# Row variances on one Trainium2 core: larger first loads, smaller last pieces, and part of one column loaded over 15 to 1 partitions

## Chip, cores and metric

The kernel runs on one core of a Trainium2 chip. The metric is the device time of one execution in microseconds; lower is better. Three runs of the kernel before took 165.55, 165.44 and 165.35 us, median 165.44 us. One more execution was recorded by the hardware profiler; its trace is what the rest is read from.

## What is computed

```python
# x: float32 (32, 512, 1024)
mean_sq = np.mean(x**2, axis=-1)
sq_mean = np.mean(x, axis=-1)**2
return (mean_sq - sq_mean).astype(np.float32)     # (32, 512)
```

So each of 16384 rows of 1024 floats gives its variance. The input has 67.11 MB and must be read once; the output has 0.07 MB.

## The kernel before, in words

The rows are laid out as 128 columns: a column is one row of 1024 floats (4 KB) in each of the 128 partitions. Columns 0 to 15 are the first 2048 rows of x (each partition holds 16 rows that follow one another in memory), columns 16 to 127 are the rest (112 rows that follow one another). A load of n columns therefore reads n x 4 KB in one stretch for each partition. All loads are issued by SyncE (SP) through `load` (L40, the DMA at L45).

**Loads.** Columns 0 to 103 come in 13 loads of 8 columns into three rotating buffers `xt` (L145); a load into a buffer in use waits for the engines that still read it. Columns 104 to 127 have a buffer of their own, `xt_end` (L73), and come in loads of 6, 6, 4, 3, 2 and 1 columns (`END_LOADS`) and then, for the last two columns, in four half columns of 2 KB a partition (L173 to L179). Loads use eight completion semaphores in turn, so that a load also waits for the one eight DMAs earlier. The two stores of results are DMAs too: the one for columns 0 to 15 goes out from ScalarE (ACT), L181, the one for the rest from SP at the end, L182.

**Work.** A column goes to one of two engines. VectorE (DVE) takes two `bn_stats` of 512 floats (L111), each of which leaves two records of count, mean and sum of squared deviations (six floats). ACT takes two passes of 1024 floats: a Copy that sums the row into `neg_mean` (L121) and a Square with that mean as its bias, which sums into the result (L129); each ends with a read of its accumulator. Of 8 columns ACT takes 3 or 2 in turn, of the last 24 those marked A in `END_WHO`. What ACT writes besides sums goes to `junk`, bf16 in SBUF.

**Joining records.** For the body and for the first two loads of the end, GpSimd (POOL) joins the DVE's records of many columns at once (`join`, L81 to L108). For later columns DVE does it itself, one `bn_aggr` a column (L169, L179). Each engine's instructions run in the order written; the framework adds the waits on semaphores.

Of the kernel before, what the change touches and what calls it, by code (L numbers as in the profile page):

```python
# [10 lines left out]
@with_exitstack  # L11
def kernel(
    ctx: ExitStack,
    tc: tile.TileContext,
    x: bass.AP,
    out: bass.AP,
):

    nc = tc.nc
    P = nc.NUM_PARTITIONS
    FP32 = mybir.dt.float32
    ACTF = mybir.ActivationFunctionType
    ALU = mybir.AluOpType

    xf = x.flatten_outer_dims()
    N, D = xf.shape
    assert N % P == 0
    ncols = N // P  # L30
    H = D // 2


    SMALL = 16
    BLOCKS = [(0, SMALL, 0), (SMALL, ncols - SMALL, SMALL * P)]

    def block_of(c):
        return next(b for b in BLOCKS if b[0] <= c < b[0] + b[1])

    def load(dst, c0, n, f0=0, f=D):  # L40

        b0, pitch, row0 = block_of(c0)
        assert c0 + n <= b0 + pitch
        ap = [[pitch * D, P], [D, n], [1, f]] if n > 1 else [[pitch * D, P], [1, f]]
        nc.sync.dma_start(  # L45
            out=dst,
            in_=dataclasses.replace(xf, offset=(row0 + c0 - b0) * D + f0, ap=ap),
        )

    def store(engine, block):  # L50
        b0, pitch, row0 = block
        engine.dma_start(
            out=dataclasses.replace(out, offset=row0, ap=[[pitch, P], [1, pitch]]),
            in_=mv[:, 1, b0 : b0 + pitch],
        )

    GROUP = 8
    NGROUPS = 13
    END0 = GROUP * NGROUPS
    ACT_OF_GROUP = (3, 2)  # L60

    END_LOADS = [6, 6, 4, 3, 2, 1]
    END_WHO = "AADDDDAADDDDDADDDADADA"
    BATCH = (2, 6, 2)

    xpool = ctx.enter_context(tc.tile_pool(name="xpool", bufs=3))
    spool = ctx.enter_context(tc.tile_pool(name="spool", bufs=4))
    opool = ctx.enter_context(tc.tile_pool(name="opool", bufs=1))

    mv = opool.tile([P, 2, ncols], FP32)  # L70
    neg_mean = opool.tile([P, ncols], FP32)
    junk = [opool.tile([P, D], mybir.dt.bfloat16, name=f"junk{i}") for i in range(4)]
    xt_end = opool.tile([P, ncols - END0, D], FP32)  # L73
    stats_of = {}

    def stats_block(name, groups, each):

        st = opool.tile([P, groups * each, 2, 6], FP32, name=name)
        return st

    def join(st, groups, each, first, step, skip):  # L81

        n = groups * each
        part = st.rearrange("p n h (e s) -> p n (h e) s", s=3)
        mean, m2 = part[:, :, :, 1], part[:, :, :, 2]
        two = opool.tile([P, n, 2], FP32, name=f"two{first}")
        mu = opool.tile([P, n, 1], FP32, name=f"mu{first}")
        dev = opool.tile([P, n, 4], FP32, name=f"dev{first}")
        g = nc.gpsimd
        g.tensor_tensor(out=two, in0=mean[:, :, 0:2], in1=mean[:, :, 2:4], op=ALU.add)  # L90
        g.tensor_tensor(out=mu, in0=two[:, :, 0:1], in1=two[:, :, 1:2], op=ALU.add)
        g.tensor_scalar(out=mu, in0=mu, scalar1=0.25, scalar2=None, op0=ALU.mult)  # L92
        g.tensor_tensor(out=dev, in0=mean, in1=mu.to_broadcast([P, n, 4]), op=ALU.subtract)  # L93
        g.tensor_tensor(out=dev, in0=dev, in1=dev, op=ALU.mult)  # L94
        g.tensor_scalar(out=dev, in0=dev, scalar1=D / 4.0, scalar2=None, op0=ALU.mult)  # L95
        g.tensor_tensor(out=dev, in0=dev, in1=m2, op=ALU.add)  # L96
        g.tensor_tensor(out=two, in0=dev[:, :, 0:2], in1=dev[:, :, 2:4], op=ALU.add)  # L97
        g.tensor_tensor(out=mu, in0=two[:, :, 0:1], in1=two[:, :, 1:2], op=ALU.add)
        var = mv[:, 1, first : first + groups * step].rearrange(
            "p (g k) -> p g k", k=step  # L100
        )[:, :, skip : skip + each]
        g.tensor_scalar(  # L102
            out=var,
            in0=mu.rearrange("p (g k) o -> p g (k o)", k=each),
            scalar1=1.0 / D,
            scalar2=None,
            op0=ALU.mult,
        )  # L108

    def dve_half(stats, h, xh):  # L110
        nc.vector.bn_stats(out=stats[:, h, :], in_=xh)  # L111

    def dve_halves(stats, xcol):
        dve_half(stats, 0, xcol[:, :H])
        dve_half(stats, 1, xcol[:, H:])

    def act_cols(cols):

        s = D ** -0.5
        for i, (xcol, c) in enumerate(cols):  # L120
            nc.scalar.activation(  # L121
                out=junk[i],
                in_=xcol,
                func=ACTF.Copy,
                scale=-s / D,
                accum_out=neg_mean[:, c : c + 1],
            )
        for i, (xcol, c) in enumerate(cols):
            nc.scalar.activation(  # L129
                out=junk[3],  # L130
                in_=xcol,
                func=ACTF.Square,
                scale=s,
                bias=neg_mean[:, c : c + 1],
                accum_out=mv[:, 1, c : c + 1],
            )

    body = []
    for par in range(2):
        groups = len(range(par, NGROUPS, 2))  # L140
        each = GROUP - ACT_OF_GROUP[par]
        body.append((stats_block(f"stats{par}", groups, each), groups, each))
    for g in range(NGROUPS):
        c0 = g * GROUP
        xt = xpool.tile([P, GROUP, D], FP32, name="xt")  # L145
        load(xt, c0, GROUP)
        skip = ACT_OF_GROUP[g % 2]
        act_cols([(xt[:, k, :], c0 + k) for k in range(skip)])
        st, _, each = body[g % 2]
        for k in range(skip, GROUP):  # L150
            dve_halves(st[:, g // 2 * each + k - skip, :, :], xt[:, k, :])
    for par, (st, groups, each) in enumerate(body):
        join(st, groups, each, par * GROUP, 2 * GROUP, ACT_OF_GROUP[par])

    nb, step, skip = BATCH
    each = step - skip
    st_end = stats_block("stats_end", nb, each)
    k = 0
    for b, n in enumerate(END_LOADS):
        load(xt_end[:, k : k + n, :] if n > 1 else xt_end[:, k, :], END0 + k, n)  # L160
        mine = range(k, k + n)
        act_cols([(xt_end[:, j, :], END0 + j) for j in mine if END_WHO[j] == "A"])
        for j in mine:
            if END_WHO[j] == "D" and b < nb:
                dve_halves(st_end[:, b * each + j - k - skip, :, :], xt_end[:, j, :])
            elif END_WHO[j] == "D":
                stats = spool.tile([P, 2, 6], FP32, name="stats")
                dve_halves(stats, xt_end[:, j, :])
                nc.vector.bn_aggr(out=mv[:, :, END0 + j], in_=stats)  # L169
        if b == nb - 1:  # L170
            join(st_end, nb, each, END0, step, skip)
        k += n
    for j in range(k, ncols - END0):  # L173
        stats = spool.tile([P, 2, 6], FP32, name="stats")
        for h in range(2):
            xh = xt_end[:, j, h * H : (h + 1) * H]
            load(xh, END0 + j, 1, h * H, H)
            dve_half(stats, h, xh)
        nc.vector.bn_aggr(out=mv[:, :, END0 + j], in_=stats)  # L179

    store(nc.scalar, BLOCKS[0])  # L181
    store(nc.sync, BLOCKS[1])  # L182
# [30 lines left out]
```

## Time and profile before

| what | value | from |
|---|---|---|
| median of three runs | 165.44 us | times |
| span of the profiled execution | 163.5 us (163.47) | page, cores view |
| median less that span: what lies around it | 1.97 us | 165.44 - 163.47 |
| DVE busy, ACT busy, POOL busy | 106.1, 94.9, 10.2 us | page, part 1 |
| queue of the loads, share of 16 DMA engines | 96.3% | page, part 3 |
| one `bn_stats` of 512 floats, alone / next start after start | 678 ns / 0.605 us | groups; 12 in 7.23 us less one tail |
| `bn_aggr` of 12 floats | 203 to 210 ns | groups |
| ACT Copy, Square, accumulator read | 1046, 1142, 186 ns | groups |
| last load landed / last instruction issued / end | 159.76 / 160.98 / 163.47 us | landings, timeline |

The page's first parts give busy time by engine and by slice. The chain of waits follows the end of the run backward to what released each step. The timeline lists instructions in order of time. The trace also keeps, for each DMA packet, its start, length and size, and for each DMA the moments at which each of the 16 DMA engines reported its share as landed; these records are called packet records and landing records below.

### The profile page before, as it was taken

Reading aid. Unit: us, or ns where it says so; the run is one execution under the profiler, and the core shown is the slowest. Engines: PE = TensorE matmul, PEld = TensorE weight load, DVE = VectorE, ACT = ScalarE, POOL = GpSimd, SP = SyncE. Lnnn points to the kernel's source line nnn. Section 1 sums busy time; section 2 is a strip of 40 time slices with the busy share of each in tenths; the row PEclk is TensorE's granted clock in tenths of the full one; section 3 lists DMA queues with packets and bytes.
Section 4 is the critical chain, followed back from the end, with each engine's and each line's share of the span. In section 5 each row is a group of like instructions: output and inputs, shape, how many; then the busy total and the mean of one; then the engine's idle time right before and its main releaser. Section 6 shows DMA issues by size and latency. Waiting matters only on the chain.

```text
span 163.5 us, 462 instructions
## 1 busy us (share of the span) xinstructions
DVE 106.1 (65%) x182; ACT 94.9 (58%) x165; POOL 10.2 (6%) x34
## 2 busy tenths in 40 slices
DVE  0008559393793917949097682949559396859993
ACT  3008756195733937349390693809755195499892
POOL 0000000000000000000000000000000635302200
DMA  7899898998999999999999999999999999999970
GB/s 257 385 481 417 385 513 385 417 481 385 481 417 385 485 409 393 497 393 425 465 393 473 417 393 505 393 401 489 393 465 425 421 391 475 391 440 409 408 291 14
DMA packets 3602, 67.19 MB, mean 411 GB/s; under 512 B 656, under 2 KB 656, under 8 KB 1296
## 3 DMA queue, kind: packets, MB, share of 16 engines
q1 hardware_dynamic: 3456, 67.17, 96.3%
q10 hardware_dynamic: 144, 0.01, 0.1%
q14 instruction: 2, 0.02, 0.0%
HBM read 67.11 MB, written 0.07 MB: 411 GB/s over the span
## 4 chain that ended last, share of the span: by engine, by line
DMA 79%; DVE 11%; ACT 8%; issue 0%; SPq 0%
DMA xt<-in_x_dram 62%; DMA xt_end<-in_x_dram 17%; DVE stats L111 10%; ACT junk L129 4%; ACT junk L121 4%; DVE mv L179 0%; SPq L45 0%
## 5 line engine op out<-in xcount | busy, mean ns | idle before, releaser
L111 DVE BATCH_NORM_STATS2 stats<-xt 128x6 f32<-128x512 f32 x142 | 85.5, 678 | 50.7 <-DMA xt<-in_x_dram 50.7
L121 ACT ACTIVATE junk<-xt 128x1024 bf16<-128x1024 f32 x33 | 34.5, 1046 | 59.2 <-DMA xt<-in_x_dram 59.2
L129 ACT ACTIVATE junk<-xt,neg_mean 128x1024 bf16<-128x1024 f32 x33 | 37.7, 1142 | 0.6
L111 DVE BATCH_NORM_STATS2 stats_end<-xt_end 128x6 f32<-128x512 f32 x16 | 9.7, 680 | 3.7 <-DMA xt_end<-in_x_dram 3.7
L121 ACT ACTIVATE junk<-xt_end 128x1024 bf16<-128x1024 f32 x8 | 8.4, 1046 | 5.0 <-POOL mv L102 4.2
L111 DVE BATCH_NORM_STATS2 stats<-xt_end 128x6 f32<-128x512 f32 x16 | 10.1, 666 | 0.1
L129 ACT ACTIVATE junk<-xt_end,neg_mean 128x1024 bf16<-128x1024 f32 x8 | 9.2, 1144 | 0.2
L90 POOL TENSOR_TENSOR two<-stats 128x72 f32<-128x72 f32 (+1 forms) x2 | 0.8, 406 | 131.3 <-DVE stats L111 131.3
L129 ACT ACTIVATION_READ_ACCUMULATOR junk<-xt,neg_mean 128x1 f32 x33 | 6.2, 186 | 0.0
L121 ACT ACTIVATION_READ_ACCUMULATOR junk<-xt 128x1 f32 x33 | 6.2, 186 | 0.0
L121 ACT ACT_TABLE_LOAD x1 | 1.3, 1283 | 0.7 <-PEq L197 0.7
L121 ACT ACTIVATION_READ_ACCUMULATOR junk<-xt_end 128x1 f32 x8 | 1.5, 186 | 0.0
L129 ACT ACTIVATION_READ_ACCUMULATOR junk<-xt_end,neg_mean 128x1 f32 x8 | 1.5, 186 | 0.0
L95 POOL TENSOR_SCALAR dev<-dev 128x144 f32<-128x144 f32 (+2 forms) x3 | 1.4, 472 | 0.3
L169 DVE BATCH_NORM_AGGREGATE mv<-stats 128x2 f32<-128x12 f32 x6 | 1.2, 203 | 0.1
L94 POOL TENSOR_TENSOR dev<-dev 128x144 f32<-128x144 f32 (+2 forms) x3 | 1.1, 362 | 0.2
L96 POOL TENSOR_TENSOR dev<-dev,stats 128x144 f32<-128x144 f32 (+1 forms) x2 | 1.1, 528 | 0.2
L93 POOL TENSOR_TENSOR dev<-stats,mu 128x144 f32<-128x144 f32 (+1 forms) x2 | 0.9, 470 | 0.2
L102 POOL TENSOR_SCALAR mv<-mu 128x36 f32<-128x36 f32 (+2 forms) x3 | 0.9, 287 | 0.3
L92 POOL TENSOR_SCALAR mu<-mu 128x36 f32<-128x36 f32 (+2 forms) x3 | 0.9, 284 | 0.3
L97 POOL TENSOR_TENSOR two<-dev 128x72 f32<-128x72 f32 (+2 forms) x3 | 0.8, 276 | 0.2
L90 POOL TENSOR_TENSOR two<-stats_end 128x16 f32<-128x16 f32 x1 | 0.2, 233 | 8.9 <-DVE stats_end L111 8.9
(9 smaller groups left out, 2.7 us busy)
## 6 DMA issues: line engine op xcount, KB each, us to landing
xt<-in_x_dram SPq DMA_DIRECT2D x13, 4096.0 KB, 22.2
xt_end<-in_x_dram SPq DMA_DIRECT2D x2, 3072.0 KB, 32.2
xt_end<-in_x_dram SPq DMA_DIRECT2D x1, 2048.0 KB, 40.0
xt_end<-in_x_dram SPq DMA_DIRECT2D x1, 1536.0 KB, 43.2
xt_end<-in_x_dram SPq DMA_DIRECT2D x1, 1024.0 KB, 45.1
xt_end<-in_x_dram SPq DMA_DIRECT2D x4, 256.0 KB, 15.3
xt_end<-in_x_dram SPq DMA_DIRECT2D x1, 512.0 KB, 36.7
out_dram<-mv SPq DMA_DIRECT2D x1, 56.0 KB, 1.6
```

Source lines behind the costliest of these rows:

```text
L90: g.tensor_tensor(out=two, in0=mean[:, :, 0:2], in1=mean[:, :, 2:4], op=ALU.add)
L92: g.tensor_scalar(out=mu, in0=mu, scalar1=0.25, scalar2=None, op0=ALU.mult)
L93: g.tensor_tensor(out=dev, in0=mean, in1=mu.to_broadcast([P, n, 4]), op=ALU.subtract)
L94: g.tensor_tensor(out=dev, in0=dev, in1=dev, op=ALU.mult)
L95: g.tensor_scalar(out=dev, in0=dev, scalar1=D / 4.0, scalar2=None, op0=ALU.mult)
L96: g.tensor_tensor(out=dev, in0=dev, in1=m2, op=ALU.add)
L97: g.tensor_tensor(out=two, in0=dev[:, :, 0:2], in1=dev[:, :, 2:4], op=ALU.add)
L102: g.tensor_scalar(out=var, in0=mu.rearrange("p (g k) o -> p g (k o)", k=each), scalar1=1.0 / D, scalar2=None, op0=ALU.mult,)
L111: nc.vector.bn_stats(out=stats[:, h, :], in_=xh)
L121: nc.scalar.activation(out=junk[i], in_=xcol, func=ACTF.Copy, scale=-s / D, accum_out=neg_mean[:, c : c + 1],)
L129: nc.scalar.activation(out=junk[3], in_=xcol, func=ACTF.Square, scale=s, bias=neg_mean[:, c : c + 1], accum_out=mv[:, 1, c : c + 1],)
L169: nc.vector.bn_aggr(out=mv[:, :, END0 + j], in_=stats)
```

## The change

Five loads now have 16 columns (the first has 15, because column 0 is treated apart), in three rotating buffers of 16 columns that hold the end as well. Loads of 8, 8, 6, 6, 5 (as 4 and 1, across two buffers), 4, 3, 2, 2 and 1 columns follow. The last three columns come in pieces: two halves; two halves, the first of which ACT works on; and 512, 256, 128 and 128 floats. ACT's half yields a third kind of record (count from a `memset`, mean, sum of squared deviations) that DVE's `bn_aggr` takes together with DVE's own two. Seven eighths of column 0 (896 floats) come in a load of their own behind the first; the last eighth (128 floats, 512 bytes a partition) comes in 16 loads over 15, 14, ... 2, 1 and 8 partitions, strung between the first five loads. ACT's discarded output goes to PSUM in f32 through four buffers in turn. POOL joins in two batches (50 and 21 columns). ACT takes 45 columns and a half instead of 41.

```diff
-    GROUP = 8
-    NGROUPS = 13
-    ACT_OF_GROUP = (3, 2)
-    END_LOADS = [6, 6, 4, 3, 2, 1]
-    END_WHO = "AADDDDAADDDDDADDDADADA"
+    FIRST = 1
+    BATCHES = [
+        ["AAAAAJJJJJJJJJJ"] + ["AAAAAAJJJJJJJJJJ"] * 4,
+        ["AAAJJJJJ"] * 2 + ["AAJJJJ"] * 2 + ["AAJJJ"],
+        ["ADDD", "ADD", "AD", "AD", "D"],
+    ]
+    PIECES = [
+        [(512, "D"), (512, "D")],
+        [(512, "A"), (512, "D")],
+        [(512, "D"), (256, "D"), (128, "D"), (128, "D")],
+    ]
+    PARTS = [[15, 14, 13], [12, 11, 10], [9, 8, 7, 6], [5, 4, 3, 2], [1, 8]]
+    SLOT = 16
...
-    junk = [opool.tile([P, D], mybir.dt.bfloat16, name=f"junk{i}") for i in range(4)]
+    junk = [ppool.tile([P, D], FP32, name=f"junk{i}") for i in range(4)]
...
+            if b == 0 and parts:
+                if i == 0:
+                    load(col0[:, :Q], 0, 1, 0, Q)
+                for n_ in parts.pop(0):
+                    load(col0[p0 : p0 + n_, Q:], 0, 1, Q, D - Q, p0, n_)
+                    p0 += n_
...
+    for pieces, rec in zip(PIECES, records):
+        xt, k = slot(c)
+        f0 = r = 0
+        for f, w in pieces:
+            xh = xt[:, k, f0 : f0 + f]
+            load(xh, c, 1, f0, f)
+            if w == "D":
+                nc.vector.bn_stats(
+                    out=rec[:, r : r + 2, :].rearrange("p r s -> p (r s)"), in_=xh
+                )
+                r += 2
+            else:
+                act(xh, ACTF.Copy, scale=1.0 / f, accum_out=rec[:, r, 1:2])
+                act(xh, ACTF.Square, scale=-1.0, bias=rec[:, r, 1:2], accum_out=rec[:, r, 2:3])
+                r += 1
+            f0 += f
+        nc.vector.bn_aggr(out=mv[:, :, c], in_=rec.rearrange("p r s -> p (r s)"))
+        c += 1
```

## The prediction

> **What bounds the kernel now.** I first read the page's DMA lines, then the chain of waits, then the timeline of the tail. From the page:
>
> ```profile
> DMA  7899898998999999999999999999999999999970
> ...
> q1 hardware_dynamic: 3456, 67.17, 96.3%
> ...
> q14 instruction: 2, 0.02, 0.0%
> ```
>
> The DMA engines are busy in every slice between first and last; the loads' queue alone fills 96.3% of sixteen engines' span. DVE (65%) and ACT (58%) have slack. The q14 line matters later. The end of the chain of waits:
>
> ```profile
> 108.32 21.83 DMA xt<-in_x_dram
> 130.15 0.02 issue
> 130.17 27.64 DMA xt_end<-in_x_dram
> 157.81 0.02 issue
> 157.83 1.38 DVE stats L111 x2
> 159.21 0.02 issue
> 159.24 0.21 DVE mv L179
> ```
>
> Up to 157.81 us the chain is loads; what appears as ACT or DVE earlier frees a buffer while two loads are still queued. So the time is start, stream, tail, and an edit counts only if it shortens the stream on the DMA engine that ends last, or the work behind the last landing. The tail:
>
> ```profile
> 155.86 1.06 ACT L121 ACTIVATE junk<-xt_end 128x1024 bf16<-128x1024 f32 x1
> ...
> 156.83 0.18 ACT L121 ACTIVATION_READ_ACCUMULATOR junk<-xt_end 128x1 f32 x1
> 157.04 1.15 ACT L129 ACTIVATE junk<-xt_end,neg_mean 128x1024 bf16<-128x1024 f32 x1
> ...
> 158.10 0.19 ACT L129 ACTIVATION_READ_ACCUMULATOR junk<-xt_end,neg_mean 128x1 f32 x1
> ...
> 159.36 1.23 DVE L111 BATCH_NORM_STATS2 stats<-xt_end 128x6 f32<-128x512 f32 x2
> 160.41 0.18 ACT L129 ACTIVATION_READ_ACCUMULATOR junk<-xt_end,neg_mean 128x1 f32 x1
> 160.63 0.21 DVE L179 BATCH_NORM_AGGREGATE mv<-stats 128x2 f32<-128x12 f32 x1
> 160.98 0.35 SPq L52 DMA_DIRECT2D out_dram<-mv  x1
> ```
>
> By the landing records the last half column landed at L = 159.76, so DVE ends 160.84 - 159.76 = 1.08 us behind L; store and end take a further 2.63 to 163.47. All sums are against this span; the median of the runs is 1.97 above it, and I add differences to 165.44.
>
> **Price of a packet.** In the packet records a row of a partition is one packet: 32 KB takes 1213 ns, 16 KB 611, 8 KB 313, 4 KB 161, 2 KB 84 to 87, and each load ends on each engine with a 4-byte packet of 9 ns. Between 32 and 2 KB that is 36.75 ns a KB (27.2 GB/s an engine) and some 9 ns a packet whatever its size. An engine carries 8 packets of each load of 128 partitions.
>
> **Part 1, sizes of loads.** Before: 23 loads, 184 packets an engine. After: 25 loads of 128 partitions (15 columns, column 0's seven eighths, four of 16, eleven from 8 down to 1, eight pieces), so 200 packets if a 60 or 64 KB row is still one. That is +16 x 9 + 2 x 9 = +0.16 us: the large loads save 39 packets, the pieces and col0 spend more. No row shows a packet above 32 KB. If such rows are cut in two, 40 packets more cost +0.36. I take one packet, as every row here is one at any size, and keep +0.36 for the range.
>
> **Part 2, column 0's eighth.** It leaves the even load: 8 x 512 B = 4 KB an engine, -0.15 us. Back come parts of 512 B: 18.8 + 9 ns, plus 9 for the closing packet, 37 ns on each engine that takes part (bounds: a 448-byte store packet took 25 ns, a 2 KB one 84). With part 1 an engine gains 0.01 us, plus 37 ns for each part that it carries. If n partitions use n engines always counted from the same one, the sixteen engines carry 16, 15, ... 10, 9, 7, 6, ... 1, 0 parts, so between +0.01 and +0.60. Only the engine that ends last decides. In the landing records the sixteen lie within 0.41 us until 41.9, and within 1.11 from 62 us to the end: 14 within 0.33, one 0.36 behind these, one 0.81. Between lie two q14 packets of 8192 B, at 55.84 and 57.08 us, of 309 and 324 ns. So two engines are late through fetches of instructions, one by about its fetch, the other by some 0.4 more that no row explains. No row gives their places. I take the middle, 8 parts: +0.30 + 0.01 = **+0.31**. Both fetches come again (DVE and ACT had run 50 to 56 instructions then; after, they reach that in the third load, near 65 us). Of the unexplained 0.4 I let half recur: **-0.20**. Stream: +0.11.
>
> The Trainium skill (DMA: Bandwidth & Descriptors, "Latency and other measured facts") calls DMA engines 7 and 15 usually slower than the others, which it ties to another kind of queue. It fits two late engines here, whose numbers the trace doesn't give. If it held, they would carry 9 and 0 parts, and the stream without the recurrence term would change by +0.01 if 15 is the later, by +0.35 if 7 is.
>
> Against evening out by index: the last store's landing records span 0.17 us over the sixteen engines, so a start in order of index explains little of a 0.6 us staircase.
>
> **Part 3, the tail.** Landings by packets, back from L: the 128s 0.23 each, the 256 0.38, halves 0.675 (the spacing before). So 127's half lands at L-0.84, 126's DVE half at L-1.52, ACT's half at L-2.19. ACT needs 2.43 us from Copy's start to the second accumulator read for 1024 floats. For 512 I go linearly from the one-element read of 186 ns: Copy less 0.43, Square less 0.48, so 1.52 (bounds: half, 1.22, and all, 2.43). ACT ends at L-2.17+1.52 = L-0.65. DVE's own half of 126 is done at L-0.83, so the new wait falls on `bn_aggr` of 126: L-0.62. Behind it in DVE's order stand all four `bn_stats` of 127, the first of which starts at L-0.50. Pitches: 512 floats 0.605; between that and 12 floats at 0.12 (aggregate to next start), 256 give 0.36 and 128 give 0.23. Sum 0.605 + 0.36 + 2 x 0.23 = 1.43, with 0.06 of drain and 0.21 of aggregate 1.70. DVE ends at L+1.20 against L+1.08: **+0.12**. The smaller last pieces hence give nothing: DVE holds a whole column's work when they land. Low bound: no wait on ACT (start L-0.68) and pitches proportional (1.48 in all), L+0.80, -0.28; high bound: ACT at 2.43, +1.03.
>
> **Parts that cost nothing.** ACT's output to PSUM, 4.5 columns more on ACT and larger buffers are hidden by the stream: a 16-column load takes about 19.4 us, ACT's six columns 6 x 2.3 = 13.9, DVE's ten 12.1. SP's order: a load waits for the DMA eight before it and for its buffer. By my reckoning 16-column loads land near 21, 41.6, 61, 80.5, 100; the fourth is issued at 41.7, needed at 61; the fifth at 61.5 (it stands behind a part that waits for the third), needed at 80.5; the 8-column ones at 80.6 and 94.5, needed at 100 and 109.8. The pieces' issues wait for loads that land 3 us or more ahead of need. Were a cover gone, each us of lateness would cost one. POOL's first join has 50 columns, not 36 (127.77 to 132.33 before): about 7.5 us from 113.5, to 121. ACT's store waits there, and behind it ACT's three columns that land at 119.5 lose 1.5 us; their buffer isn't reused. POOL's one `memset` stands ahead of everything.
>
> **Sum.** +0.11 + 0.12 = +0.23: 165.44 + 0.23 = **165.67 us**. A measurement here tells about 0.2% (0.33 us) from no change, so the forecast is no change.
>
> **Rivals.**
> - *The late engine carries many parts.* Place: the low end of the staircase. From 11 parts on (0.01 + 11 x 0.037 - 0.20 + 0.12 = 0.34) the change is slower; at 16, +0.52: 165.96; with rows cut in two as well 166.3. For: no row puts the late engine elsewhere; against: six of sixteen places. Chance 0.36, with the cut rows.
> - *The lateness is gone.* If neither late engine recurs beyond the pack, the end is set by the staircase, up to 0.6 + 0.33 behind the first, against 1.11: -0.2 to -0.5 on the stream; with the tail at its lower bound 164.7 to 165.1. For: the 0.4 is one event; against: the fetches do recur. Chance 0.23.
> - *The parts don't spread.* The trace shows no DMA of less than 128 partitions. All 128 pieces on one engine would take 128 x 28 + 16 x 9 ns = 3.7 us: up to 169. Chance 0.03. The skill's same page ("Why a DMA increments its semaphore by 16 and not by 1") states that the largest count up to 16 that divides the partitions is used, lowest numbers first: n engines for n partitions; no row shows it.
>
> The forecast's own case, no change, has 0.38. Faster 0.23, same 0.38, slower 0.39 (the first and third rival). The forecast's own range is 165.1 to 165.8; the wanted range goes from 164.9 (lateness gone, half of the tail's low bound) to 166.3 (many parts and cut rows).
>
> **What would show it.** Right: landing spacing of 16-column loads of 19.4 us without gaps; the last landing 0.0 to 0.3 later than 159.76; a wait of DVE on ACT in front of 126's aggregate; DVE's end 1.1 to 1.3 behind L. Wrong: packets of 32 KB in the large loads; DVE idle when the last 128 floats land; a DMA line with holes; sixteen landings within 0.5 us at the end.

## The result and the profile after

The changed kernel takes 167.45 us (median of four runs, 167.38 to 167.84) against 165.50 for the kernel before on the same chip: ratio 1.0112, 95% interval 1.0091 to 1.0134. It is 1.95 us slower; the forecast of 165.67 and the range to 166.3 were too low. The profiled execution has a span of 165.7 us, 2.2 above that of before; it is the slowest of the four runs by 0.3 to 0.5 us, so the causes are held against the differences between medians, and the trace says where these arise.

From the page of after, the lines that answer to those of before:

```profile
DMA  7999595998999699799989969999999999999940
...
q1 hardware_dynamic: 4000, 67.17, 95.5%
...
q14 instruction: 3, 0.02, 0.0%
```

The stream still fills the span: it is not starved by late loads or buffers (the dips to 5 and 7 are a way of counting: packets are booked in the slice where they start, and a packet of 64 KB lasts 2.42 us, over half a slice). Two things differ. The packets of the loads' queue went from 3456 to 4000, and the instruction queue shows **three** packets where before shows two.

The last pieces of the chain of waits of after (start, length, what):

```profile
114.84 27.02 DMA xt<-in_x_dram
141.87 0.02 issue
141.88 17.57 DMA xt<-in_x_dram
159.46 0.02 issue
159.48 0.73 ACT junk L85 x2
160.21 0.02 issue
160.24 0.69 ACT junk L85
160.93 0.13 ACTq L254
161.06 0.04 DVEq L224
161.09 0.04 issue
161.14 0.20 DVE mv L224
161.34 1.29 DVE rec L214 x4
162.62 0.02 issue
162.65 0.27 DVE mv L224
```

As forecast, the end runs through ACT's half of column 126, DVE's aggregate that waits for it, and the four pieces of column 127. But it begins later, and is longer. In the landing records the last load lands at L = 161.41 (before: 159.76), DVE ends 1.50 us behind it (before: 1.08), and store and end take 2.78 (before: 2.63): 1.65 + 0.42 + 0.15 = 2.2 us.

Where the 1.65 arises is seen best in how the sixteen DMA engines finish each load. From the packet records: the median end of the fourteen early ones, and how far the two late ones lie behind it. (`all undone` is the experiment below that keeps only the 16-column loads.)

```
end of load            after                  all undone
third of 16 columns    60.83  +0.31  +0.35    60.60  +0.24  +0.65
fourth                 80.25  +1.26  +1.32    80.04  +0.56  +0.90
last of 4 columns     144.87  +1.31  +1.43   144.43  +0.54  +0.98
last landing          161.41                 159.72
```

In the fourth load, at 66 us, come the two fetches of instructions (packets of 8192 B on the instruction queue); there two engines fall behind the other fourteen (the pack), as in before. In after both stand 1.3 to 1.4 us behind the pack, and the last landing is 15.11 us after the later one's end of the 4-column load, against 14.32. The third packet of the instruction queue, at 150.30 us, falls in between: it is on the engine that was already last, and takes it from 1.43 to 2.13 us behind the pack.

### The profile page after: what moved, and what is told of

Same layout as the page of the kernel before. It is cut to its first block, busy times and chain, and to the rows that moved or that the text cites. A ratio compares the mean times of both kernels' runs of the same rounds, so it can differ in the third digit from the quotient of the medians.

```text
span 165.7 us, 501 instructions
## 1 busy us (share of the span) xinstructions
DVE 101.0 (61%) x179; ACT 102.2 (62%) x185; POOL 9.4 (6%) x33
## 4 chain that ended last, share of the span: by engine, by line
DMA 87%; ACT 8%; DVE 1%; issue 1%; SPq 1%; ACTq 0%; DVEq 0%
DMA xt<-in_x_dram 74%; DMA col<-in_x_dram 13%; ACT junk L85 8%; DVE rec L214 1%; SPq L63 1%; DVE mv L224 0%; ACTq L254 0%; DVEq L224 0%; ACTq L85 0%
## 5 line engine op out<-in xcount | busy, mean ns | idle before, releaser
L134 DVE BATCH_NORM_STATS2 st<-xt 128x6 f32<-128x512 f32 x142 | 85.2, 677 | 57.7 <-DMA xt<-in_x_dram 57.7
L85 ACT ACTIVATE junk<-xt 128x1024 f32<-128x1024 f32 (+1 forms) x46 | 46.1, 1002 | 57.9 <-DMA xt<-in_x_dram 57.8
L85 ACT ACTIVATE junk<-xt,neg_mean 128x1024 f32<-128x1024 f32 x45 | 49.5, 1100 | 0.1
L134 DVE BATCH_NORM_STATS2 one<-xt 128x6 f32<-128x512 f32 x16 | 10.0, 669 | 3.6 <-DMA xt<-in_x_dram 3.6
L85 ACT ACTIVATION_READ_ACCUMULATOR junk<-xt 128x1 f32 x46 | 8.6, 186 | 0.0
L85 ACT ACTIVATION_READ_ACCUMULATOR junk<-xt,neg_mean 128x1 f32 x45 | 8.4, 187 | 0.0
L214 DVE BATCH_NORM_STATS2 rec<-xt 128x6 f32<-128x512 f32 (+2 forms) x7 | 3.3, 512 | 0.0
L122 POOL TENSOR_SCALAR mv<-mu 128x10 f32<-128x10 f32 (+3 forms) x10 | 2.1, 238 | 0.2
L139 DVE BATCH_NORM_AGGREGATE mv<-one 128x2 f32<-128x12 f32 x9 | 1.8, 204 | 0.2
L134 DVE BATCH_NORM_STATS2 one<-col 128x6 f32<-128x512 f32 x2 | 1.4, 676 | 0.0
```

Source lines behind the costliest of these rows:

```text
L85: nc.scalar.activation(out=junk[njunk % len(junk)][:, : xcol.shape[1]], in_=xcol, func=func, **kw)
L122: g.tensor_scalar(out=mv[:, 1, c0 : c0 + m], in0=mu[:, at : at + m, 0], scalar1=1.0 / D, scalar2=None, op0=ALU.mult,)
L134: nc.vector.bn_stats(out=st[:, h, :], in_=xcol[:, h * H : (h + 1) * H])
L139: nc.vector.bn_aggr(out=mv[:, :, c], in_=st1)
L214: nc.vector.bn_stats(out=rec[:, r : r + 2, :].rearrange("p r s -> p (r s)"), in_=xh)
```

## Experiments

All medians are given as differences from the kernel before on the same chip, since that moved between 165.50 and 165.68. "Third fetch" is the third packet of 8192 B on the instruction queue. L is the time of the last landing.

**Fewer columns on ACT.**

```diff
-        ["AAAAAJJJJJJJJJJ"] + ["AAAAAAJJJJJJJJJJ"] * 4,
-        ["AAAJJJJJ"] * 2 + ["AAJJJJ"] * 2 + ["AAJJJ"],
+        ["AAAAJJJJJJJJJJJ"] + ["AAAAAJJJJJJJJJJJ"] * 4,
+        ["AAJJJJJJ", "AAAJJJJJ"] + ["AAJJJJ"] * 2 + ["AAJJJ"],
```

> The changed kernel with six columns fewer on ACT (39.5 in place of 45.5; DVE takes them in the 16-column loads and the first 8-column one). After has three packets of 8192 B on the instruction queue where before has two; the third, at 150.30 us, comes when ACT has run 176 instructions, and before's ACT has 172 in all. Theory (third fetch): ACT stays below that count, the packet at 150 us goes, and the last landing comes 0.7 us earlier (0.31 the packet, 0.37 the stretched packet beside it): median 166.75 against 167.45. Rival (only parts, pieces and tail cost): no change, 167.4.

Measured 166.80, +1.26: 0.69 less than after. The packet at 150.30 us is gone; a third comes at 161.18, behind the last landing at 160.47, so it was moved and not removed. The size agrees with the theory, but this kernel alone doesn't prove it: its first two fetches moved as well, from 66 us to 53.5 and 87.7 us; L came 0.95 earlier, not 0.7; and DVE, with six columns more, ended 1.80 us behind L, not 1.50.

**Column 0 not apart.** The first load has 16 columns, DVE takes column 0 among those that POOL joins.

```diff
-    FIRST = 1
+    FIRST = 0
-        ["AAAAAJJJJJJJJJJ"] + ["AAAAAAJJJJJJJJJJ"] * 4,
+        ["AAAAAJJJJJJJJJJJ"] + ["AAAAAAJJJJJJJJJJ"] * 4,
-                if i == 0:
-                    load(col0[:, :Q], 0, 1, 0, Q)
-                for n_ in parts.pop(0):
-                    load(col0[p0 : p0 + n_, Q:], 0, 1, Q, D - Q, p0, n_)
-                    p0 += n_
-            dve_col(col0, 0)
```

> The changed kernel with column 0 back in the first load (16 columns, DVE takes column 0, POOL joins it), no load of seven eighths and no parts. In the packet records of after the two late engines run four and two parts behind the third 16-column load and one behind the fifth load, so they carry 15 and 13 of the 16. Theory (late engines carry the parts): 15 x 0.037 = 0.56 and 0.08 for the extra load go, 0.15 of bytes come back: -0.48, median 166.95. Rival (the parts fill idle time on engines that are not last): no change, 167.4.

Measured 166.07, +0.53: 1.42 less than after, three times the theory's 0.48. The late engines do carry the parts, but that price doesn't explain all. In this kernel the third fetch is still there, at 149.50 us, and the last landing is at 160.01, only 0.26 behind before's. The packet records show two parts of the gain: the last engine ends the 4-column load at 145.43, 0.88 earlier than in after, and the third fetch falls on the engine that is only 0.59 behind the pack, so that it adds 0.16 to the last end and not 0.70.

**The end as before.**

```diff
-        ["ADDD", "ADD", "AD", "AD", "D"],
+        ["ADDD", "ADD", "AD", "AD", "D", "D"],
-        [(512, "D"), (512, "D")],
-        [(512, "A"), (512, "D")],
-        [(512, "D"), (256, "D"), (128, "D"), (128, "D")],
+        [(512, "D"), (512, "D")],
+        [(512, "D"), (512, "D")],
```

> The changed kernel with the end as before: column 125 in one load, columns 126 and 127 in halves that DVE takes, no ACT record. Theory (pieces): three loads fewer, 24 x 9 + 27 ns = -0.24 on the stream, and the tail behind the last landing back from 1.51 to 1.08 us, -0.43: median 166.8. Rival (the tail is DVE's work on a whole column either way): -0.24 alone, 167.2.

Measured 166.49, +0.95: 1.00 less than after, but not for the reason given. DVE ends 1.62 us behind the last landing, not 1.08: the tail was not restored at all. The gain lies in the stream (L at 160.72), where the third fetch has moved from 150.30 to 159.86 and stretches no packet, and behind DVE's end, where store and end take 2.54 and not 2.78.

**Before with more columns on ACT.**

```diff
-    ACT_OF_GROUP = (3, 2)
+    ACT_OF_GROUP = (4, 2)
```

> The kernel before with seven columns more on ACT (4 of 8 in place of 3 in the groups with an even number), so that ACT passes 176 instructions; nothing else changes, DVE has seven columns fewer. Theory (third fetch): a third packet of 8192 B on the instruction queue near 150 us, on an engine that is already late, last landing 0.3 to 0.7 us later: 166.0 against 165.5. Rival (columns on ACT are hidden by the stream): 165.5.

Measured 165.46, -0.08, ratio 0.9996 (0.9987 to 1.0005): no change, though the third fetch came. From its page:

```profile
q14 instruction: 3, 0.02, 0.0%
```

It lies at 149.13 us, when ACT had run 173 to 177 instructions, and stretched one packet by 0.37 us. The last landing is at 159.88, 0.12 later than before's. The packet records say why: at the end of the 4-column load one engine is 0.51 behind the pack and the other 1.03. The fetch falls on the first of these, which has half a microsecond to give. So the third fetch by itself costs next to nothing; the theory, as I had put it, fell. What remains is a joint one: the fetch costs when the engine that it hits is the last, or level with the last, as in after (+1.31 and +1.43).

**All three together, large loads kept.** 41 columns on ACT as before.

> The three edits together: 41 columns on ACT as before, no parts and no load of seven eighths, end in a whole column 125 and four halves on DVE. What is left of the change are the five loads of 16 columns, the shared buffers and junk in PSUM. If the price is in packets alone: 160 packets an engine against 184 before and 20 loads against 23, -0.25 us, so 165.3 against 165.54. If the three savings measured so far (0.65, 1.38, 0.96) add up: 164.5. If the 16-column loads themselves cost: above 165.5.

Measured 165.80, +0.12, ratio 1.0011 (1.0002 to 1.0020). The savings don't add up (0.69 + 1.42 + 1.00 would be 3.1 of 1.95), as they must not if they share one cause. And although each engine runs 16 packets fewer than in before (168 against 184; the expectation counted one load too few), nothing is won: L is at 159.72, but DVE ends 1.67 us behind it.

**The eighth of column 0 in one even load.**

```diff
-    PARTS = [[15, 14, 13], [12, 11, 10], [9, 8, 7, 6], [5, 4, 3, 2], [1, 8]]
+    PARTS = [[128]]
```

> The changed kernel with the eighth of column 0 in one load over 128 partitions in place of 16 loads over 15 to 1; the load of seven eighths stays. Each engine has 8 packets of 512 B and one closing packet, 0.23 us. Theory (late engines carry 15 and 13 parts of 37 ns, 0.48 to 0.56): 167.45 - 0.29 = 167.15. Rival (many small loads cost more than their packets, by slowing the large packets beside them): most of the 1.38 that went with the parts goes, 166.2 to 166.5.

Measured 166.48, +0.80: 1.15 less than after, four times the theory's 0.29 and within what the rival gave. Its two late engines are 0.67 and 0.96 behind the pack at the 4-column load, whose last end, 145.52, is 0.79 earlier than in after; the third fetch, at 149.53, stretches a packet on the nearer one by 0.37 and adds 0.39 to the last end, not 0.70.

**No record from ACT.**

```diff
-        [(512, "A"), (512, "D")],
+        [(512, "D"), (512, "D")],
```

> The changed kernel with the first half of column 126 on DVE as well, all loads unchanged. In after DVE starts 126's half at 160.25, 1.5 us behind the first half of 125, and waits 0.25 us for ACT before 126's aggregate. Theory (DVE is behind anyway, the record relieves it): 0.61 more on DVE, 0.25 of waiting gone, +0.35: 167.8. Rival (the wait on ACT is what lengthens the tail): -0.25, 167.2.

Measured 167.12, +1.44: 0.51 less than after. The rival's sign, but not its reason: DVE ends 1.59 us behind the last landing against 1.50. From its timeline (start, length, engine, line, operation):

```profile
158.59 1.23 DVE L214 BATCH_NORM_STATS2 rec<-xt 128x6 f32<-128x512 f32 x2
159.73 0.19 DVE L224 BATCH_NORM_AGGREGATE mv<-rec 128x2 f32<-128x12 f32 x1
159.84 0.64 DVE L214 BATCH_NORM_STATS2 rec<-xt 128x6 f32<-128x512 f32 x1
160.51 0.21 DVE L224 BATCH_NORM_AGGREGATE mv<-rec 128x2 f32<-128x12 f32 x1
160.64 1.35 DVE L214 BATCH_NORM_STATS2 rec<-xt 128x6 f32<-128x512 f32 x4
162.03 0.27 DVE L224 BATCH_NORM_AGGREGATE mv<-rec 128x2 f32<-128x24 f32 x1
```

DVE works without a pause through 126 and 127; the record on ACT neither relieves nor delays by more than a tenth. What changed is L, 160.70 against 161.41, with the same loads: without the half column ACT has 194 instructions and not 198, and the third fetch comes at 159.81, not at 150.30. The first two come at 65.69 and 65.83, almost as in after, so this pair shows the third fetch best: of the 0.71, 0.19 stands already at the end of the 4-column load (146.12 against 146.31), and the rest arises behind it.

**Large loads undone as well.** As the kernel with all three edits, but:

```diff
-        ["AAAAAJJJJJJJJJJJ"] + ["AAAAAJJJJJJJJJJJ"] * 4,
+        ["AAJJJJJJ", "AAAJJJJJ"] * 5,
```

> As the kernel with the three edits, but its first 80 columns in ten loads of 8 columns, two to a buffer. 40 packets and 5 closing packets more, +0.40 by the 9 ns a packet. Rival (packets of 64 KB run 18 ns over their bytes at 27.2 GB/s in after, packets of 32 KB 11.6 ns in before, so one large packet saves 5 ns and not 9 over two small): 40 x 5 + 45 ns = +0.25.

Measured 166.41, +0.73: 0.61 more than with loads of 16. By the medians the large loads are a gain, a larger one than either theory gave. In the packet records a row of 64 KB is one packet of 2418 ns, two rows of 32 KB are 2 x 1213; that is 0.32 us for 40 packets. The two profiles show less: L is at 159.91 against 159.72, 0.19 later, and store and end take 2.81 against 2.60. So the traces show 0.19 of it in the stream, and the rest I can't place.

**Column 125 back on ACT.** As the kernel with all three edits, but:

```diff
-        ["AAAJJJJJ"] * 2 + ["AAJJJJ"] * 2 + ["AAJJJ"],
-        ["ADDD", "ADD", "AD", "AD", "D", "D"],
+        ["AAJJJJJJ", "AAAJJJJJ"] + ["AAJJJJ"] * 2 + ["AAJJJ"],
+        ["ADDD", "ADD", "AD", "AD", "D", "A"],
```

> The kernel with all three edits, but column 125 on ACT (as in before) and one column of the first 8-column load on DVE in return. The last landing of that kernel is where before has it (159.72 against 159.75), yet DVE ends 1.67 us behind it and not 1.08. Theory (DVE takes 124 and 125 in a row and is a column behind when the last halves land): DVE's tail falls to 1.1, -0.57: 0.45 us below before, 165.2 where before is 165.65. Rival (the tail is the two last columns' own work): no change, before + 0.1.

Measured 165.03, -0.51, ratio 0.9972 (0.9961 to 0.9984): faster than both kernels, by 0.3% against before. The tail of the kernel with all three edits, where DVE takes 124 and 125, then of this one:

```profile
157.40 1.23 DVE L133 BATCH_NORM_STATS2 one<-xt 128x6 f32<-128x512 f32 x2
158.54 0.68 DVE L200 BATCH_NORM_STATS2 rec<-xt 128x6 f32<-128x512 f32 x1
...
159.25 1.23 DVE L200 BATCH_NORM_STATS2 rec<-xt 128x6 f32<-128x512 f32 x2
...
160.50 0.64 DVE L200 BATCH_NORM_STATS2 rec<-xt 128x6 f32<-128x512 f32 x1
161.18 0.21 DVE L210 BATCH_NORM_AGGREGATE mv<-rec 128x2 f32<-128x12 f32 x1
```

```profile
156.97 1.03 ACT L84 ACTIVATE junk<-xt 128x1024 f32<-128x1024 f32 x1
157.12 0.21 DVE L138 BATCH_NORM_AGGREGATE mv<-one 128x2 f32<-128x12 f32 x1
157.66 1.35 DVE L200 BATCH_NORM_STATS2 rec<-xt 128x6 f32<-128x512 f32 x2 [0.33 <-DMA xt<-in_x_dram]
...
159.17 1.23 DVE L200 BATCH_NORM_STATS2 rec<-xt 128x6 f32<-128x512 f32 x2
159.21 0.19 ACT L84 ACTIVATION_READ_ACCUMULATOR junk<-xt,neg_mean 128x1 f32 x1
160.44 0.21 DVE L210 BATCH_NORM_AGGREGATE mv<-rec 128x2 f32<-128x12 f32 x1
```

In the first, DVE has column 125's two halves at 157.40 and starts 126 only at 158.54, with work waiting from there to the end. In the second ACT has 125 (156.97 on), DVE stands idle for 0.33 us until 126's first half lands at 157.66, and ends 1.08 us behind the last landing (159.57), as in before.

**The parts even, and the parts on eight engines.** As after, but `PARTS = [[16, 16], [16, 16], [16, 16], [16], [16]]`, then `PARTS = [[8, 8, 8], [8, 8, 8], [8, 8, 8, 8], [8, 8, 8, 8], [8, 8]]`.

> The changed kernel with the eighth of column 0 in eight loads of 16 partitions: each engine should carry 8 packets of 512 B and 8 closing packets, 0.30 us, 0.07 more than in the one even load. By packets: 0.07 above that kernel, which was 0.80 above before: before + 0.87. Rival (what costs is many small loads between the large ones, whoever carries them): half of the way back to the changed kernel or more, before + 1.4 to + 1.9.

> The changed kernel with the eighth of column 0 in sixteen loads of 8 partitions: the first eight engines carry 16 parts each, the others none. The late engines then carry 16 in place of 15 and 13, +0.04 to +0.11 us: before + 2.0 to 2.1. Rival (the number of loads counts, not who carries them): as the changed kernel, before + 1.95. Rival (engines out of step slow each other): clearly more, before + 2.3 or above.

Measured 166.63, +1.09, and 167.53, +1.99. Even parts in eight loads cost 0.29 more than the one even load (0.07 by packets); the sixteen parts on eight engines cost what the staircase costs, 1.95. That looks as if what counts were who carries the parts, but the packet records say something else. The last engine ends the 4-column load at 146.08 with even parts and at 146.32 with parts on eight engines, only 0.24 apart. The rest of the 0.90 is the third fetch. With even parts (149.99 us) it finds the engine that is 0.55 behind the pack while the other is 1.24 behind, and adds nothing to the last end; with parts on eight engines it finds the later of two that are level, 1.30 and 1.34, and adds 0.67. There the last landing is at 161.41, as in after.

**Column 0 apart, nothing else.** The end in halves as in the third experiment, and ACT's columns as before:

```diff
-        ["AAAAAJJJJJJJJJJ"] + ["AAAAAAJJJJJJJJJJ"] * 4,
+        ["AAAAAJJJJJJJJJJ"] + ["AAAAAJJJJJJJJJJJ"] * 4,
```

> The kernel with all three edits, with column 0's load of seven eighths and the 16 parts put back: no third fetch, end in halves. If the price of the parts stands by itself: before + 0.12 + 1.38 = before + 1.5. If the parts and the third fetch cost so much because they meet on the same late engine: the same 1.5 in which the fetch has no share, since the late engines stay late without it. If it needs the third fetch: before + 0.7 or less.

Measured 167.05, +1.51, the number of the first case. But this kernel isn't free of a third fetch, as I had expected: one comes at 156.63 us, and two packets of 4 KB take 499 and 487 ns in place of 160. Up to the end of the 4-column load the late engine is at 144.72 + 1.19 = 145.91, against 144.43 + 0.98 = 145.41 in the kernel with all three edits: +0.50. By packets it is 0.41: this engine carries two parts between the fourth and the fifth large load, so it is the one with 13 parts, 0.48, with the load of seven eighths 0.08 and the bytes -0.15. Both stretched packets are on the engine that is already last, in the last load of a whole column: it goes from 1.18 to 2.16 us behind the pack, +0.97. So the agreement with +1.5 is luck, and the price of the parts doesn't stand by itself: 0.50 of it does, and the rest is a fetch on the last engine.

The same reading of the packet records for the kernels with 16-column loads (us; "behind" is behind the median of the pack, "fetch adds" is what the end of the last engine moved against the pack from the 4-column load to the first 2 KB pieces):

| kernel | two late engines behind, 4-column load | last end there | fetch adds | L |
|---|---|---|---|---|
| all three edits | 0.54, 0.98 | 145.41 | none comes | 159.72 |
| column 0 not apart | 0.59, 1.13 | 145.43 | 0.16 | 160.01 |
| one even load | 0.67, 0.96 | 145.52 | 0.39 | 160.35 |
| even parts | 0.55, 1.24 | 146.08 | 0.00 | 160.55 |
| no record from ACT | 0.95, 1.29 | 146.12 | 0.00 | 160.70 |
| column 0 apart, nothing else | 1.04, 1.19 | 145.91 | 0.97 | 161.14 |
| parts on eight engines | 1.30, 1.34 | 146.32 | 0.67 | 161.41 |
| after | 1.31, 1.43 | 146.31 | 0.70 | 161.41 |

In each row L less the last end and less what the fetch adds is 14.3 to 14.6 us, so these two account for L to within 0.3.

**The steps from before to after.** Five of these kernels stand in a row, each a small edit from the next, and their differences sum to the whole:

| kernel | against before | step |
|---|---|---|
| 16-column loads, 125 on ACT | -0.51 | |
| 125 on DVE | +0.12 | +0.63, tail (0.59) |
| column 0 apart, four columns more on ACT | +0.95 | +0.83, stream |
| pieces for 125 and 127 | +1.44 | +0.49, not in L or the tail |
| half of 126 on ACT (the change) | +1.95 | +0.51, third fetch 9.5 us earlier |

The third row takes two edits together. By themselves they are +1.39 (column 0 apart, with the fetch on the last engine at 156.63) and -0.56 (four columns more on ACT, with the fetch at 159.86, where it stretches no packet): what a step is worth depends on where it moves the fetch. In the fourth row the two profiles have L at 160.72 and 160.70 and DVE's end 1.62 and 1.59 behind it; only store and end differ, 2.54 and 2.78. So the traces show 0.2 of that step, and not in the stream.

## Why the prediction was wrong

**What bounds the kernel** was right: the stream on the engine that ends last, and the tail. No load came too late, rows of 60 and 64 KB are single packets (the case taken), and 512-byte packets take 25 to 32 ns, 27 as a rule (28 forecast). (The prediction's 36.75 ns a KB is for 1000 bytes; a KB of 1024 bytes, as everywhere else here, takes 37.6.)

**Part 1, sizes of loads,** forecast +0.16 in all, as the sum of fewer large packets and more small ones. The signs were right. By the medians both sizes were low: loads of 16 columns bring 0.61, where packets give 0.36 to 0.40, and the step with the pieces costs 0.49, where packets give 0.24. In L the profiles show only 0.19 of the first and nothing of the second.

**Part 2 failed.** The stream was forecast 0.11 longer; the last landing was 1.65 later. "I take the middle, 8 parts" was the first mis-sized term: the late engines are the second and the fourth of the staircase. In the packet records the two late chains run four and two 512-byte parts between the fourth and the fifth large load, where parts of 5, 4, 3 and 2 partitions stand, and one each behind the fifth, where 1 and 8 stand; that is 15 and 13 parts in all. (The stretches that these fill on the late engines, 122 and 63 to 65 ns, are the same in the three other kernels with the staircase in which both engines were late by then.) The rival "the late engine carries many parts" was the case, at its upper end, as far as the parts go: by packets 15 of them come to 0.49 with the load of seven eighths and the bytes, and the last engine ends the 4-column load at 145.91 to 146.35 in the kernels with the staircase, 145.25 to 145.43 in those with 16-column loads and column 0 not apart. The Trainium skill (DMA: Bandwidth & Descriptors, "Latency and other measured facts") calls DMA engines 7 and 15 usually slower, which it ties to another kind of queue; those would carry 9 and 0 parts. Here the parts that the late engines carry say second and fourth, and the measurement decides. "Of the unexplained 0.4 I let half recur, -0.20" was the second: the two fetches came again, close together (65.98 and 66.04 us), and stretched packets of 64 KB by 0.66 and 0.61 us. The 0.4 "that no row explains" stood in the packet records of before: beside its two fetches, packets of 32 KB took 1461 and 1875 ns in place of 1213, 0.25 and 0.66 more.

**"4.5 columns more on ACT are hidden by the stream" failed** in a way that the busy time doesn't show. Each column on ACT is four instructions, and in the kernels with 197 or more instructions on ACT a third fetch comes at 149 to 150 us, when ACT has run some 176. I had noted the count at the first fetches (50 to 56) and not asked for the next. In after the engine that it hits is itself the last, so that there is no slack: the fetch adds 0.70, most of the +0.79 us between the 4-column load and the last landing (15.11 against 14.32), and the kernel that differs only in the half column is 0.51 faster. In before with more columns on ACT the same fetch costs 0.12 us in L, and nothing that the medians show. That there was no slack is due to the parts only in part. On the engine that the fetch hits, a packet was stretched by 0.61 at 66 us; in the three kernels with the staircase and both early fetches near 66 us where one of the stretches was shorter, 0.45 to 0.53, the two late engines stand 0.15 to 0.35 apart, in after 0.12. How a fetch meets a packet is chance as far as these profiles, one for each kernel, can tell. The Trainium skill (Runtime: NRT & Kernel Launch, "Instruction fetch mechanics") calls the cost of such a fetch mostly hidden; here it is paid on the DMA engine that carries the packet, in a kernel that waits for that engine, and the measurement decides.

**Part 3, the tail,** forecast +0.12, DVE's end 1.20 behind L; it was 1.50. The step from ACT's Copy to its second read was 1.57 (1.52 forecast), DVE's last five instructions 1.67 (1.70 forecast). What failed was the spacing back from L: the last two pieces landed 0.17 apart each, not 0.23, 127's first half at 160.69, L - 0.72 instead of L - 0.84, and ACT's half of 126 at 159.46, L - 1.95 instead of L - 2.19. So ACT ended, and DVE began its last four pieces, 0.3 closer to L. More than that, I laid the tail of before beside it and didn't see what makes that one short. Its last whole column, 125, is on ACT, while the change has DVE take 124 and 125. From the timeline of before, the Copy of column 125:

```profile
158.19 1.04 ACT L121 ACTIVATE junk<-xt_end 128x1024 bf16<-128x1024 f32 x1
```

Moving that one column is worth 0.63 us, in the kernel with all three edits.

**What stays open.** Whose instructions the third fetch brings in the kernels with fewer than 197 on ACT (156.63, 159.81, 159.86 and 161.18 us; all four are kernels with 16 parts); whether parts between large loads slow other engines' packets besides (64 KB packets take 15 to 28 ns more than their bytes at 27.2 GB/s with the staircase, 12 to 15 without it and with the even load, in one profile each, so the ranges meet); how much of the two engines' lateness is due to the parts and how much to the stretch of the early fetches; and the part of the 0.61 (large loads) and of the 0.49 (pieces) that the profiles don't show.

## What to carry to other kernels

When a kernel is bound by its DMA stream, find the one DMA engine that ends last and ask of each edit what it adds there: evening out bytes by position costs time if the late engines are those that get more. Instructions are also DMA traffic: see when the instruction queue's packets come, and whether the DMA engine that they land on has slack. A third fetch added 0 to 0.97 us here, by whether it fell on the engine that was last; so a small edit can gain or lose half a microsecond for a reason that isn't in the edit, and a difference in medians is to be followed into the packet records before it is called the edit's price. And in the tail, look at which engine has the last whole column before the last pieces, before cutting the pieces smaller.

## What was not expected of the hardware

A packet of 8192 B on the instruction queue takes 309 to 387 ns while the stream runs and in most cases lengthens a data packet beside it by 0.25 to 0.66 us, so that two of sixteen engines stay 0.5 to 1.4 us behind for the rest of the run. In after and in three experiments with the staircase they are the same two in the order of the parts, the second and the fourth. A row of 64 KB goes as one packet of 2418 ns.
